# Second norm of the last tile on one engine, four scatters later, and routing products moved by a unit

## The chip, the cores and the metric

The kernel runs on one core of a Trainium2 chip. The metric is the device time of one launch in microseconds (us): the median of the runs before the change is 1239.01 us. The engines are named as the profile names them: PE is TensorE's matrix products (PEld its weight loads), DVE is VectorE, ACT is ScalarE, POOL is GpSimd, and SP is the engine that only issues transfers.

## The reference

One decoder block on 1024 tokens of width 1024, all in float32. The first half normalises, runs a state-space branch and a gated chunk branch, merges them by gates, and projects. The second half, in which the change lies, is a mixture of 32 experts in 4 groups of 8:

```python
h   = x + gate_a * (merged @ w_out)          # output projection and residual
xn  = rmsnorm(h) * (1 + scale_m) + shift_m   # the second norm
lg  = xn @ w_rg + b_rg                       # 4 group logits per token
grp = argmax(lg)                             # one group per token
le  = (xn @ w_re + b_re)[grp]                # 8 expert logits of that group
top_v, top_i = top_k(le, 2)                  # two experts per token
wgt = softmax(lg)[grp] * softmax(top_v)
y   = sum over the two of wgt * ((silu(xn @ w1) * (xn @ w3)) @ w2)
out = rmsnorm(h + gate_m * y)
```

The reference sorts the 2048 pairs of token and expert by expert, in blocks of up to 128 rows.

## The kernel before

The tokens are 8 tiles of 128. The order of the work is written by hand: a list of units, each with its matrix products; before a unit's products, every side generator in flight is advanced by one `yield`. So a `yield` puts what follows it one unit later. There is no scheduler that moves anything; each engine runs its instructions in the order in which they were issued.

The **output projection** (`out_mm`, products of lines L112 to L114: three products of rounded halves for each float32 product) runs tile after tile. A tile has two halves of 512 columns of 24 products each. Tiles 2 to 5 have two units each (one per half), tile 6 four units of 12 products, tile 7 eight units of 6. When a half is complete, `out_read` adds it to the residual on VectorE (h, L87), and `h_half` squares it on ScalarE (L1340) and multiplies it by a row on GpSimd (L87, xn<-h). After the second half, `norm2` joins the side generators.

**norm2(j)** turns the tile by PE transposes (L1355; ScalarE copies them, L105), forms the reciprocal root r on VectorE, and multiplies the turned tile by the router's weights (L1372: the 36 logits). For the rows themselves it scales by r on ScalarE (L1375, two halves) and adds the shift on GpSimd (L87, xn<-xn, two halves), and ScalarE's queue stores the rows to DRAM (L1377, xrows), from where the experts gather them.

**route(tiles)** runs once for each pair of tiles in `GROUPS`: VectorE finds the group, the two experts and a mask `mb` from the logits; after WAIT[0] yields PE forms the running count of each expert (L1464, L1466, L1467), which needs the mask; VectorE and GpSimd form one-hot rows (`ohr`); after WAIT[1] yields PE multiplies them (L1493), and VectorE adds the result to the table of lists in SBUF and keeps the column sums (`cum`). Last, `scatter` writes one row for each choice and token to a table in DRAM by four indirect transfers of GpSimd (L1507). For the last pair the scatters are put in `late_rows` and issued after the third gather of the experts. That table is read only by a loop for overflowing experts at the end of the kernel.

**The experts** start with two gathers of rows (L1675) and the turn of the first of them (L1690), then the third gather, then `late_rows`. Sixteen experts have up to 128 rows and sixteen up to 64; their weights come from DRAM by loads of up to 2 MB (wexp), are rounded by ScalarE (L108, ewh) and completed by VectorE (L87, ewl).

Of the kernel before, what the change touches and what calls it, by code (L numbers as in the profile page):

```python
# [14 lines left out]
AF = mybir.ActivationFunctionType  # L15
OP = mybir.AluOpType
# [8 lines left out]
NJ = 8  # L25
# [27 lines left out]
def hybrid_block(ctx: ExitStack, tc: tile.TileContext, ins, out):  # L53
    nc = tc.nc
    V, A, G, T = nc.vector, nc.scalar, nc.gpsimd, nc.tensor
# [15 lines left out]
    def k4(nm, shape, dt=F32):  # L71
        return pool.tile([P] + shape, dt, name=name(nm), tag="k4", bufs=N4)
# [4 lines left out]
    def tmp(nm, shape, dt=F32, bufs=2):  # L77
        return pool.tile(shape, dt, name=name(nm), tag=nm, bufs=bufs)
# [4 lines left out]
    def ps_aux():  # L83
        return psum.tile([P, 512], F32, name=name("aux"), tag="aux", bufs=4)

    def tt(o, a, b, op, eng=V):
        eng.tensor_tensor(out=o, in0=a, in1=b, op=op)  # L87

    def stt(o, a, s, b, op0, op1, **kw):
        V.scalar_tensor_tensor(out=o, in0=a, scalar=s, in1=b, op0=op0, op1=op1, **kw)  # L90

    def ts(o, a, s1, s2=None, op0=OP.mult, op1=None, eng=V):
        if op1 is None:
            eng.tensor_scalar(out=o, in0=a, scalar1=s1, scalar2=None, op0=op0)
        else:
            eng.tensor_scalar(out=o, in0=a, scalar1=s1, scalar2=s2, op0=op0, op1=op1)
# [7 lines left out]
    def act_copy(o, a):  # L104
        A.activation(out=o, in_=a, func=AF.Copy)  # L105
# [34 lines left out]
    def rsqrt(o, a, n):  # L140
        for _ in rsqrt_steps(o, a, n):
            pass
# [898 lines left out]
    rowv = {}  # L1041
# [272 lines left out]
    def load_next(q=nc.sync, later=None):  # L1314
        if loaded[0] < len(order):
            key = loads[loaded[0]]
            raws[key] = w_load(key[0], expert_of(key[1]), q, whole[key], later, not is_l(key[1]), key)
            loaded[0] += 1
# [27 lines left out]
    def norm2(j):  # L1346

        ht, x2 = hts[j], x2s[j]
        tiles = next(g for g in GROUPS if j in g)
        B = len(tiles)  # L1350

        def turn(hf):
            ps = ps_aux()
            for k in range(4):
                T.transpose(ps[:, k * P:(k + 1) * P], hres[j][:, (4 * hf + k) * P:(4 * hf + k + 1) * P], ident)  # L1355
            o = ht[:, 4 * hf:4 * hf + 4].rearrange("p k c -> p (k c)")
            if j == NJ - 1 and hf == 0:
                V.tensor_copy(out=o, in_=ps)
            else:
                act_copy(o, ps)  # L1360

        turn(0)
        ms, r = nrm[:, j, 3:4], nrm[:, j, 4:5]
        ts(nrm[:, j, 2:3], nrm[:, j, 0:1], 1.0 / DM, RMS_EPS, OP.mult, OP.add)
        stt(ms, nrm[:, j, 1:2], 1.0 / DM, nrm[:, j, 2:3], OP.mult, OP.add)
        rsqrt(r, ms, 1)
        yield
        turn(1)
        yield
        lps = ps_aux()  # L1370
        for k in range(KD):
            T.matmul(out=lps[:, 0:36], lhsT=ht[:, k], rhs=rk["wr"][:, k], start=(k == 0), stop=(k == KD - 1))  # L1372
        for hf in range(2):
            hs = slice(hf * 512, (hf + 1) * 512)
            A.activation(out=x2[:, hs], in_=x2[:, hs], func=AF.Identity, scale=r)  # L1375
            tt(x2[:, hs], x2[:, hs], rowv[3][:, hs], OP.add, G)
        nc.scalar.dma_start(out=xrows[j * P:(j + 1) * P, :], in_=x2)  # L1377
        if j == NJ - 1:
            load_next(nc.scalar, nc.gpsimd)
        yield  # L1380
        if j == tiles[0]:
            groups[tiles] = k4("rt", [DM])
        L = groups[tiles][:, 0:36 * B].rearrange("p (t n) -> p t n", t=B)
        stt(L[:, j - tiles[0]], lps[:, 0:36], r, rk["cb"], OP.mult, OP.add)
        if j == tiles[-1]:
            yield from route(tiles, L)

    late_rows = []
    WAIT = {(4, 5): (2, 2), (6,): (4, 2)}
    GROUPS = ((0, 1), (2, 3), (4, 5), (6, 7))  # L1390

    def route(tiles, L):
# [63 lines left out]
        tt(mb, mk[:, 0], mk[:, 1], OP.add)  # L1456
        for _ in range(WAIT.get(tiles, (1, 1))[0]):
            yield
# [26 lines left out]
        for q, t in pairs:  # L1485
            gts(rhs[:, q, t, 0], mk[:, q, t], ids[:, t:t + 1])
            ts(oh[:, q, t], rk["iota"], pos[:, q, t:t + 1], None, OP.is_equal)
            ts(rhs[:, q, t, 1], mk[:, q, t], wv[:, q, t:t + 1], None, OP.mult)
        for _ in range(WAIT.get(tiles, (1, 1))[1]):
            yield  # L1490
# [14 lines left out]
        def scatter():  # L1505
            for q, t in pairs:
                ins_ = G.indirect_dma_start(out=table[:, :], out_offset=bass.IndirectOffsetOnAxis(ap=adi[:, q, t:t + 1], axis=0),  # L1507
                                            in_=row[:, q, t], in_offset=None, bounds_check=NT * NEXP - 1, oob_is_err=False)
                for prev in scatters:
                    tc.declare_no_dep(ins_.ins, prev.ins, reason="each token and choice has its own row")  # L1510
                scatters.append(ins_)
        for t in range(B):
            tt(cum, cum, mb[:, t], OP.add)
        if tiles[-1] >= NJ - 2:
            late_rows.append(scatter)
        else:
            scatter()
# [13 lines left out]
    def out_read(j, n):  # L1531
        ns = slice(n * 512, (n + 1) * 512)
        tt(hres[j][:, ns], hres[j][:, ns], ops[j, n], OP.add)
        h_half(j, n)
        if n == 1:
            h_store(j)
            side.append(norm2(j))
# [440 lines left out]
    with tc.For_i(0, n_any, 1):  # L1978
        y_add(x_index(NEXP - 1), yos[NEXP - 1][:, 0:512], hbuf_h)
        with tc.For_i(0, NEXP, 1) as e:  # L1980
            n_0 = nc.values_load(sm["sti"][:, bass.ds(e, 1)], min_val=1, max_val=2, skip_runtime_bounds_check_because=why)
            n_b = nc.values_load(nxi[0:1, bass.ds(e, 1)], min_val=1, max_val=NB, skip_runtime_bounds_check_because=why)
            with tc.For_i(n_0, n_b, 1) as b:
                tcol = tmp("tcol", [P, 2], I32, bufs=1)
                for h in range(2):
                    nc.sync.dma_start(out=tcol[HALF * h:HALF * (h + 1)],
                                      in_=tview[bass.ds(b, 1), :, bass.ds(e, 1), :].rearrange("b p e w -> p (b e w)"))
                xi = tmp("xi", [P, 1], I32, bufs=1)
                hf = tmp("hf", [P, 1], bufs=1)
# [55 lines left out]
```

## Time and profile before

| what | value |
|---|---|
| median of 3 runs | 1239.01 us (1237.97 to 1239.11) |
| profiled execution | 1239.78 us, its span 1238.1 us |
| granted TensorE clock, mean | 0.965 |
| PE busy | 1133.7 us, 92% of the span |
| DVE busy | 735.2 us, 59% |
| ACT busy | 463.2 us, 37% |
| POOL busy | 377.6 us, 30% |
| DMA, mean | 253 GB/s |

Times in the rows are microseconds from the start of the span. A row in order of time has the start, the duration, the engine, the line, the operation with its output and inputs, and the number of instructions that were joined to it; in brackets stands how long the engine was idle before and what released it. [...] The output projection ends at 647.7 us; from 666.58 us the experts run.

### The profile page before, as it was taken

What the parts mean: (1) busy time and instruction counts of PE and PEld (TensorE: products, weight loads), DVE (VectorE), ACT (ScalarE), POOL (GpSimd) and SP (SyncE); (2) the same over time, 40 slices, a digit from 0 to 9 for tenths busy, and PEclk for the clock granted to TensorE, in tenths of its full rate; (3) what the DMA queues carried; (4) which work ended last, traced back from release to release, by engine and by line L of the source; (5) the groups of instructions that cost most, each with busy time, mean ns of one, the idle gap of its engine ahead of it and who ended that gap; (6) DMA issues with size and microseconds to landing.
All of it is one profiled execution on the core that took longest, in us unless ns stands there. A gap on an engine that the chain in (4) does not pass through costs nothing. (4 is left out here: it accounts for less than half of the span.)

```text
span 1238.1 us, 16769 instructions
## 1 busy us (share of the span) xinstructions
PE 1133.7 (92%) x6237; PEld 872.7 (70%) x6238; DVE 735.2 (59%) x1223; ACT 463.2 (37%) x664; POOL 377.6 (30%) x477
## 2 busy tenths in 40 slices
PE   4998999999999999999995999999898999898980
PEld 4897888888878888788774776666565666665630
DVE  4614562568597555656668976666464566565616
ACT  6422233234215421034324754444342444443303
POOL 2799273533000211415565111111111111111210
PEclk9999999999999999999897999999899998999995
DMA  9711122583541155545466999999999999998986
GB/s 333 222 35 58 62 86 57 197 289 102 190 151 52 35 190 175 185 166 219 152 229 241 339 353 396 401 402 404 406 400 404 388 397 377 380 394 310 381 301 271
DMA packets 106663, 313.44 MB, mean 253 GB/s; under 512 B 21035, under 2 KB 59527, under 8 KB 91858
## 3 DMA queue, kind: packets, MB, share of 16 engines
q1 hardware_dynamic: 92520, 274.14, 58.6%
q0 software_dynamic: 9088, 20.32, 6.3%
q10 hardware_dynamic: 4970, 17.88, 3.7%
q8 instruction: 50, 0.82, 0.3%
q14 instruction: 35, 0.29, 0.1%
HBM read 287.02 MB, written 33.83 MB: 259 GB/s over the span
## 5 line engine op out<-in xcount | busy, mean ns | idle before, releaser
L87 DVE TENSOR_TENSOR ewl<-wexp,ewh 128x1024 fp32r<-128x1024 f32 x176 | 207.8, 1221 | 82.0 <-ACT ewh L108 79.8
L108 ACT ACTIVATE ewh<-wexp 128x1024 fp32r<-128x1024 f32 x176 | 174.3, 1053 | 38.8 <-DMA wexp<-in_w 36.3
L112 PE MATMUL mm<-xn,wh 128*128 128x512 f32 x320 | 127.4, 398 | 0.0
L114 PE MATMUL mm<-xn,wl 128*128 128x512 f32 x320 | 125.1, 391 | 0.0
L113 PE MATMUL mm<-xn,wh 128*128 128x512 f32 x320 | 125.0, 391 | 0.0
L87 DVE TENSOR_TENSOR wl<-wraw,wh 128x1024 fp32r<-128x1024 f32 x38 | 55.0, 1456 | 110.5 <-ACT wh L108 110.5
L1741 PE MATMUL mm<-wexp,xs 128*64 128x256 f32 x992 | 115.4, 382 | 3.9 <-DMA wexp<-in_w 3.6
L1675 POOL DMA_INDIRECT xg<-xrows,w x29 | 30.7, 1060 | 282.8 <-PE aux L1690 128.6
L113 PE MATMUL mm<-ewl,xth 128*128 128x512 f32 x256 | 103.2, 403 | 0.7 <-DVE ewl L87 0.7
L1741 PEld LDWEIGHTS mm<-wexp,xs 128*64 128x64 f32 x992 | 69.0, 137 | 48.9 <-issue 9.1
L112 PE MATMUL mm<-ewh,xth 128*128 128x512 f32 x256 | 102.3, 400 | 0.2 <-ACT xth L108 0.2
L114 PE MATMUL mm<-ewh,xtl 128*128 128x512 f32 x256 | 100.5, 393 | 0.0
L1725 POOL DMA_INDIRECT hbuf<-yo,w x28 | 52.8, 1887 | 123.1 <-DVE yo L87 109.7
L798 ACT ACTIVATE gate<-mm,vcol 128x512 f32<-128x512 f32 x32 | 22.0, 688 | 134.7 <-PE mm L114 134.7
L112 PE MATMUL mm<-ewh,w 128*128 128x512 f32 x128 | 55.9, 437 | 17.7 <-ACT ewh L108 17.7
L112 PEld LDWEIGHTS mm<-xn,wh 128*128 128x128 f32 x320 | 60.4, 189 | 13.7 <-issue 1.6
L114 PEld LDWEIGHTS mm<-xn,wl 128*128 128x128 f32 x320 | 60.2, 188 | 12.8
L113 PEld LDWEIGHTS mm<-xn,wh 128*128 128x128 f32 x320 | 60.4, 189 | 11.8
L87 DVE TENSOR_TENSOR yo<-mm,macc 128x512 f32<-128x512 f32 (+1 forms) x64 | 42.7, 686 | 41.6 <-PE mm L1741 37.5
L108 ACT ACTIVATE w<-aux 128x512 fp32r<-128x512 f32 x16 | 9.6, 597 | 140.5 <-PE aux L1709 140.5
L113 PEld LDWEIGHTS mm<-ewl,xth 128*128 128x128 f32 x256 | 48.3, 189 | 19.3 <-DVE ewl L87 10.1
L108 ACT ACTIVATE wh<-wraw 128x1024 fp32r<-128x1024 f32 x38 | 39.6, 1052 | 58.6 <-PE mm L113 29.6
(369 smaller groups left out, 2454.1 us busy)
## 6 DMA issues: line engine op xcount, KB each, us to landing
wexp<-in_w SPq DMA_DIRECT2D x76, 2048.0 KB, 25.5
wexp<-in_w SPq DMA_DIRECT2D x48, 512.0 KB, 12.0
wadr<-in_w_ada SPq DMA_DIRECT2D x32, 512.0 KB, 4.8
wexq<-in_w SPq DMA_DIRECT2D x24, 512.0 KB, 9.1
wada<-in_w_ada SPq DMA_DIRECT2D x8, 1024.0 KB, 11.2
wraw<-in_w_gate SPq DMA_DIRECT2D x16, 512.0 KB, 3.8
gate<-gate ACTq DMA_DIRECT2D x16, 512.0 KB, 2.8
gin<-gate SPq DMA_DIRECT2D x16, 512.0 KB, 3.8
```

The source lines that it names most:

```text
L87: eng.tensor_tensor(out=o, in0=a, in1=b, op=op)
L108: A.activation(out=hi, in_=raw, func=AF.Copy)
L112: T.matmul(out=ps, lhsT=lh, rhs=rh, start=first, stop=False)
L113: T.matmul(out=ps, lhsT=lh, rhs=rl, start=False, stop=False)
L114: T.matmul(out=ps, lhsT=ll, rhs=rh, start=False, stop=last)
L798: A.activation(out=box["g"][:, sl], in_=box[hf], func=AF.Sigmoid, bias=col("bg", 8 * s + d))
L1675: G.indirect_dma_start(out=xg, out_offset=None, in_=rows[:, :], in_offset=bass.IndirectOffsetOnAxis(ap=xi, axis=0), bounds_check=rows.shap ...
L1725: G.indirect_dma_start(out=rows[:, :], out_offset=bass.IndirectOffsetOnAxis(ap=yi, axis=0), in_=yo, in_offset=None, bounds_check=rows.shap ...
L1741: T.matmul(out=ps[sl, 0:n], lhsT=xt[:, k, HALF * h:HALF * (h + 1)], rhs=w[:, n * g:n * (g + 1)], start=(kt == 0), stop=(kt == nk - 1), til ...
```

## The change

Three edits. The last tile's second norm is finished by one VectorE operation, (x2 * r) + shift over 128x1024, in place of two scalings on ScalarE and two adds on GpSimd. The entry of WAIT for the pair (2, 3) is new: its running-count products come one unit later and its one-hot products two; the one-hot products of the pair (4, 5) come one unit later. (The entry for (6,) named no group and had no effect.) The four scatters of the pair (4, 5) join those of the pair (6, 7) in `late_rows`.

```diff
--- before.py
+++ after.py
@@ -1370,10 +1370,14 @@
         lps = ps_aux()
         for k in range(KD):
             T.matmul(out=lps[:, 0:36], lhsT=ht[:, k], rhs=rk["wr"][:, k], start=(k == 0), stop=(k == KD - 1))
-        for hf in range(2):
-            hs = slice(hf * 512, (hf + 1) * 512)
-            A.activation(out=x2[:, hs], in_=x2[:, hs], func=AF.Identity, scale=r)
-            tt(x2[:, hs], x2[:, hs], rowv[3][:, hs], OP.add, G)
+        if j == NJ - 1:
+
+            stt(x2, x2, r, rowv[3], OP.mult, OP.add)
+        else:
+            for hf in range(2):
+                hs = slice(hf * 512, (hf + 1) * 512)
+                A.activation(out=x2[:, hs], in_=x2[:, hs], func=AF.Identity, scale=r)
+                tt(x2[:, hs], x2[:, hs], rowv[3][:, hs], OP.add, G)
         nc.scalar.dma_start(out=xrows[j * P:(j + 1) * P, :], in_=x2)
         if j == NJ - 1:
             load_next(nc.scalar, nc.gpsimd)
@@ -1386,7 +1390,7 @@
             yield from route(tiles, L)
 
     late_rows = []
-    WAIT = {(4, 5): (2, 2), (6,): (4, 2)}
+    WAIT = {(2, 3): (2, 2), (4, 5): (2, 3)}
     GROUPS = ((0, 1), (2, 3), (4, 5), (6, 7))
 
     def route(tiles, L):
@@ -1511,7 +1515,7 @@
                 scatters.append(ins_)
         for t in range(B):
             tt(cum, cum, mb[:, t], OP.add)
-        if tiles[-1] >= NJ - 2:
+        if tiles[-1] >= NJ - 4:
             late_rows.append(scatter)
         else:
             scatter()
```

Behind the first edit all line numbers are 4 higher: L1464 becomes L1468, L1493 L1497, L1507 L1511.

On PE the running-count products of the pair (2, 3) stood directly behind tile 5's last product, ahead of the logits of tile 4. Before (mm is a projection product, rt_4968 the pair's routing buffer, ht a turned tile):

```order
2386 L114 MATMUL mm_5104<-wo_4431,ml_4839 128x512
2387 L1464 LDWEIGHTS before
2388 L1464 MATMUL aux_5143<-rt_4968,before 128x32
...
2396 L1467 MATMUL aux_5143<-cum,ones 128x32
2397 L1372 MATMUL aux_5171<-rk_2032,ht_4942 128x36 x8
2398 L1355 MATMUL aux_5185<-ident,h_4842 128x128 x4
2399 L112 MATMUL mm_5204<-wo_4100,mh_5005 128x512
```

And after:

```order
2386 L114 MATMUL mm_5104<-wo_4431,ml_4839 128x512
2387 L1372 MATMUL aux_5141<-rk_2032,ht_4942 128x36 x8
2388 L1355 MATMUL aux_5155<-ident,h_4842 128x128 x4
2389 L112 MATMUL mm_5174<-wo_4100,mh_5005 128x512
...
2400 L114 MATMUL mm_5174<-wo_4100,ml_5006 128x512
2401 L1468 LDWEIGHTS before
2402 L1468 MATMUL aux_5189<-rt_4968,before 128x32
...
2410 L1471 MATMUL aux_5189<-cum,ones 128x32
2411 L1355 MATMUL aux_5219<-ident,h_4842 128x128 x4
2412 L112 MATMUL mm_5174<-wo_4431,mh_5005 128x512
```

The logits of tile 4, a turn of tile 5 and twelve products of tile 6 now come first.

On ScalarE, in the same place: rt_4968 is again the pair's routing buffer, xn_685 the rows of tile 4, ht_5071 the turned tile 5, mh the rounded half of the projection's input. Before:

```order
334 L108 ACTIVATE mh_5133<-mg_3879 128x1024
335 L1459 ACTIVATE rt_4968<-rt_4968 128x8
336 L1460 ACTIVATE rt_4968<-rt_4968 128x2
337 L1375 ACTIVATE xn_685_4941<-xn_685_4941,nrm 128x512 x2
338 L1377 DMA xrows<-xn_685_4941 128x1024
339 L105 ACTIVATE ht_5071<-aux_5185 128x512
340 L105 ACTIVATE ht_5071<-aux_5242 128x512
```

And after:

```order
334 L108 ACTIVATE mh_5133<-mg_3879 128x1024
335 L1379 ACTIVATE xn_685_4941<-xn_685_4941,nrm 128x512 x2
336 L1381 DMA xrows<-xn_685_4941 128x1024
337 L105 ACTIVATE ht_5071<-aux_5155 128x512
338 L1463 ACTIVATE rt_4968<-rt_4968 128x8
339 L1464 ACTIVATE rt_4968<-rt_4968 128x2
340 L105 ACTIVATE ht_5071<-aux_5219 128x512
```

The two exponentials of the pair moved behind the scaling and the store of tile 4 and the first copy of turned tile 5; they now stand between its two copies.

On GpSimd, from the pair (2, 3)'s one-hot rows on (ohr_5149 before, ohr_5195 after); xn_685 are the rows of tile 4, xn_698 of tile 5, xn_715 before and xn_714 after those of tile 6, table the scatters. Before:

```order
286 L94 TENSOR_SCALAR ohr_5149<-rt_4968,rk_2032 128x32 x4
287 L87 TENSOR_TENSOR xn_685_4941<-xn_685_4941,macc_2838 128x512 x2
288 L1507 DMA table<-rk_2032,rt_4968 32768x2 x4
289 L87 TENSOR_TENSOR xn_715_5261<-h_5009,macc_2174 128x512
290 L87 TENSOR_TENSOR xn_698_5070<-xn_698_5070,macc_2838 128x512 x2
291 L87 TENSOR_TENSOR xn_715_5261<-h_5009,macc_2174 128x512
292 L94 TENSOR_SCALAR ohr_5366<-rt_5240,rk_2032 128x32 x4
293 L87 TENSOR_TENSOR xn_715_5261<-xn_715_5261,macc_2838 128x512 x2
294 L1507 DMA table<-rk_2032,rt_5240 32768x2 x4
295 L87 TENSOR_TENSOR xn_733_5479<-h_5137,macc_2174 128x512 x2
```

And after:

```order
286 L87 TENSOR_TENSOR xn_685_4941<-xn_685_4941,macc_2838 128x512 x2
287 L94 TENSOR_SCALAR ohr_5195<-rt_4968,rk_2032 128x32 x4
288 L87 TENSOR_TENSOR xn_714_5238<-h_5009,macc_2174 128x512
289 L87 TENSOR_TENSOR xn_698_5070<-xn_698_5070,macc_2838 128x512 x2
290 L1511 DMA table<-rk_2032,rt_4968 32768x2 x4
291 L87 TENSOR_TENSOR xn_714_5238<-h_5009,macc_2174 128x512
292 L94 TENSOR_SCALAR ohr_5366<-rt_5217,rk_2032 128x32 x4
293 L87 TENSOR_TENSOR xn_714_5238<-xn_714_5238,macc_2838 128x512 x2
294 L87 TENSOR_TENSOR xn_733_5467<-h_5137,macc_2174 128x512 x2
295 L94 TENSOR_SCALAR ohr_5555<-rt_5429,rk_2032 128x32 x4
```

The adds of tile 4 moved ahead of the one-hot rows, the pair (2, 3)'s scatters behind the adds of tile 5; the pair (4, 5)'s scatters and the adds of the last tile (xn_733) are gone from here.

## Rows read from the trace of the kernel before

**Rows 1.** TensorE's waits from 600 to 667 us (the view of waits).

```profile
PE aux L1464 <- DVE rt L87: 9.4, 3, 6.3
...
PE aux L1493 <- DVE ohr L94: 3.0, 2, 1.6
```

**Rows 2.** Stretches: length, busy PE, PEld, DVE, ACT, POOL, clock, DMA, GB/s.

```profile
600.00:620.00 20.00, 17.38 (x86) 14.99 (x84) 16.91 (x76) 5.50 (x12) 7.79 (x9) 0.83 0.53 188
...
640.00:650.00 10.00, 9.66 (x44) 7.68 (x42) 3.40 (x10) 2.02 (x5) 6.24 (x6) 0.86 0.78 279
```

**Rows 3.** TensorE in time: start, duration, operation, count, [idle before <-releaser].

```profile
592.10 1.87 PE L1372 MATMUL aux<-rk,ht 128*128 128x36 f32 x16
...
608.44 0.18 PE L1464 MATMUL aux<-rt,before 128*128 128x32 bf16 x1 [2.62 <-DVE rt L87]
...
608.57 3.46 PE L1372 MATMUL aux<-rk,ht 128*128 128x36 f32 x16
...
630.54 0.18 PE L1464 MATMUL aux<-rt,before 128*128 128x32 bf16 x1 [0.45 <-DVE rt L87]
...
637.93 1.43 PE L1493 MATMUL aux<-ohr 128*128 128x64 f32 x8 [1.57 <-DVE ohr L94]
...
639.51 0.63 PE L113 MATMUL mm<-wo,mh 128*128 128x512 f32 x1
...
647.27 0.39 PE L113 MATMUL mm<-wo,mh 128*128 128x512 f32 x1
647.50 0.40 PE L114 MATMUL mm<-wo,ml 128*128 128x512 f32 x1
...
666.58 1.94 PE L1690 MATMUL aux<-ident,xg 128*128 128x128 f32 x8 [5.38 <-DMA xg<-xrows,xidx]
```

**Rows 4.** VectorE in order of time, operations of the routing.

```profile
605.46 0.34 DVE L87 TENSOR_TENSOR rt<-rt,rk 128x8 f32<-128x8 f32 x2
...
605.97 0.42 DVE L87 TENSOR_TENSOR rt<-rt 128x8 f32<-128x8 f32 x3
...
624.01 4.48 DVE L87 TENSOR_TENSOR rt<-rt 128x8 f32<-128x8 f32 x3
...
652.75 1.37 DVE L87 TENSOR_TENSOR rt<-rt,rk 128x8 f32<-128x8 f32 x2
...
654.30 1.20 DVE L87 TENSOR_TENSOR rt<-rt 128x8 f32<-128x8 f32 x3
```

**Rows 5.** ScalarE and its queue in order of time, around 615 us.

```profile
615.08 0.33 ACTq L1377 DMA_DIRECT2D xrows<-xn  x1
615.51 0.60 ACT L105 ACTIVATE ht<-aux 128x512 f32<-128x512 f32 x1 [3.40 <-POOL xn L87]
```

**Rows 6.** GpSimd in order of time.

```profile
612.55 2.50 POOL L87 TENSOR_TENSOR xn<-xn,macc 128x512 f32<-128x512 f32 x2
...
652.77 2.50 POOL L87 TENSOR_TENSOR xn<-xn,macc 128x512 f32<-128x512 f32 x2 [2.57 <-ACT xn L1375]
...
671.51 1.01 POOL L1507 DMA_INDIRECT table<-rk,rt  x1 [0.30 <-DVE rk L90]
...
683.02 1.04 POOL L1675 DMA_INDIRECT xg<-xrows,w  x1 [6.87 <-PE aux L1690]
697.71 1.01 POOL L1675 DMA_INDIRECT xg<-xrows,w  x1 [13.65 <-PE aux L1690]
```

**Rows 7.** Transfers: issue, count, size, median us to landing.

```profile
wexp<-in_w SPq DMA_DIRECT2D x76, 2048.0 KB, 25.5
...
wexp<-in_w POOLq DMA_DIRECT2D x1, 2048.0 KB, 11.6
```

**Rows 8.** The view of the tile table, its scatters' landing.

```profile
DMA to landing us min/median/max: 2.1/5.5/8.8
```

**Rows 9.** The view of line L90 (ns min/median/max), operations of 128x1024.

```profile
L90 DVE SCALAR_TENSOR_TENSOR tail<-tail,nrm,gf x8: 1279/1280/1287, 1215.4 to 1228.5; 128x1024 f32<-128x1024 f32 x8
```

**Rows 10.** TensorE's waits from 666 to 1215 us, the largest.

```profile
PE mm L112 <- ACT ewh L108: 17.7, 8, 3.4
```

## Prediction

> **What bounds the kernel now.** I read four views, in this order. First the waits of TensorE from 600 to 667 us [rows 1]: the end of the output projection, the routing of the last tokens and the first gather. Until then TensorE runs its products back to back, so what delays it here delays the end. The reader is to see that 9.4 us go to three waits of the running-count products (L1464) for the routing mask and 3.0 us to two waits of the one-hot products (L1493). Second the table by stretches [rows 2]: beside these waits the granted clock is lost, 0.83 in 600:620 and 0.86 in 640:650, so part of each is at the lower of its two levels. Third TensorE's rows in order of time [rows 3], which tie the two together: the 2.62 us wait at 608.44 is followed by a logit product of 3.46 us where the same one took 1.87, and the 1.57 us wait at 637.93 by products of 0.63 (639.51) where they are 0.39 otherwise and start 0.23 apart (647.27, 647.50). The wait of 0.45 at 630.54 has no such tail. Fourth the rows of VectorE, ScalarE and GpSimd around these places [rows 4 to 6].
>
> After 667 us TensorE waits little: the largest item is 17.7 us for the experts' rounded weights, over 8 times [rows 10]. Loads there follow one another as buffers come free, so I take this stage to move as one block with the moment at which the first gathered rows are turned (666.58, [rows 3]). The prediction is then: how much earlier that moment comes.
>
> **The change part by part.**
>
> *Pair (2,3): its running-count products a unit later, its one-hot products two.* The 2.62 us wait at 608.44 goes, since by then twelve products stand ahead of them; the mask was ready at 608.4, and TensorE now arrives at about 610.6 (605.66, plus 1.7 for the logits, 0.4 for the turn, 12 x 0.23). With it goes the half-clock stretch behind it: 3.46 - 1.87 = 1.6 for the logits, about 0.4 for the turn, and six products of 0.63 like the one at 639.51, each some 0.2 more, = 1.2; together 3.2. So -5.8.
>
> What is late next: the logits of tile 5. They need ScalarE's copies of the turned tile, and these stand behind tile 4's store of its normed rows, which waits for GpSimd's two adds. In the trace the adds start at 612.55, after four one-hot rows of GpSimd [rows 6]; the store is issued at 615.08, and the copy runs at 615.51 [rows 5]. The change puts the adds ahead of the one-hot rows, so they should end at 613.9 to 614.5; then the store's issue (0.33), one copy (0.60), the two small exponentials that now stand between the copies (0.3, an estimate), and the second copy (0.6): 615.7 to 616.4. TensorE would be there at 610.65 + 0.4 + 2.75 = 613.8. A new wait of 1.9 to 2.6, or less if the adds overlap better; I take +2.0. I bound it by 0.9 and 2.6 (the wait that went).
>
> Does this wait bring the half clock back? Of the waits shown, 2.62 and 1.57 did, 0.45 did not. 2.0 lies among those that did; its price in rows is between 0 and 3.2. I take half, +1.6. [...]
>
> *Pair (4,5).* Its routing on VectorE comes behind the table update of pair (2,3), and that behind pair (2,3)'s one-hot products, which now run in the second half of tile 6. In the trace this routing lost 4.48 - 0.42 = 4.1 us in three small operations at 624.01, against 605.97 [rows 4], while GpSimd ran three adds of 128x512. These adds now come ahead of the pair's scatters, so most of this loss goes; but the start is held by the one-hot products. By hand: logits of tile 5 done at 617.5, twelve products and the one-hot products to 621.1, table update to 622.5, routing of some 4 to 5 us: the mask at about 627. TensorE arrives at about 625.3. The wait of 0.45 becomes about 1.75 (0 to 2.5): +1.3, from -0.45 to +2.0.
>
> Its one-hot products come six products later, 6 x 0.23 = 1.4 us. Of the 1.57 us wait about 0.5 stays, since the routing in front is no quicker: -1.1 (0 to -1.57). The half clock behind it (8 products x 0.20 = 1.6) goes with it in most cases: -1.3. Together -2.4, bounds +0.5 and -3.2.
>
> *Pair (4,5)'s scatters.* Four issues of 1.01 us, 0.30 apart (the row at 671.51), leave GpSimd before the tail and stand behind the third gather with the four that were there. Eight take 8 x 1.3 = 10.4 us from 670.2 (one spacing before that row) to 680.6. GpSimd's next work is the gather at 683.02, before which it idled 6.87: 2.4 us are left, so nothing. Without that cover each scatter would cost the gather 1.3; and even then its rows are turned only after those of the expert before, whose turn frees GpSimd at 697.71 [rows 6]. [...] In the tail an emptier GpSimd may start its first multiplication 0.3 earlier; I take 0.2, within the next term.
>
> A wait is added: VectorE's logit operation of tile 6 takes the buffer of pair (2,3)'s routing and so waits for that pair's scatters to land. They are issued from about 622 to 627, and the slowest landing in the trace is 8.8 us [rows 8]: 636 at the latest. Queued behind it are pair (4,5)'s table update and the residual adds of the last tile, which are due at about 640. So 4 us are left, and I count nothing.
>
> *The last tile's norm.* Two ScalarE scalings and two GpSimd adds (2.50 from 652.77 [rows 6]) go. They were not on the path themselves; but during the adds VectorE's routing of the last pair took 1.37 for two operations against 0.34, and 1.20 for three against 0.42 [rows 4]: 1.8 us, all of it on the path that ends the last wait of 6.3 [rows 1]. They are replaced by one VectorE operation of 128x1024 ahead of the last logits. The same form takes 1.28 us at the end of the kernel [rows 9], of which I let 0.08 overlap: +1.2. Left: -0.6, with the 0.2 above -0.8; bounds -1.1, and +1.2 if the stalls have another cause. [...]
>
> **The sum.** -5.8 + 2.0 + 1.6 + 1.3 - 2.4 - 0.8 = -4.1 us. The profiled execution took 1239.78 (span 1238.1 and 1.7 around it), so 1235.7 for its like; it lies 0.8 above the median of the runs, 1239.01, so the median after should be 1234.9.
>
> **The rivals.**
>
> 1. *The wait only moves.* The new wait before the logits of tile 5 is as long as the old (2.6), the half clock comes back whole (3.2), pair (4,5)'s wait is 2 longer and its half clock stays: -5.8 + 2.6 + 3.2 + 2.0 - 1.1 - 0.8 = +0.1; with half of these, -2. Time 1237 to 1239. For it: ScalarE's queue did wait 3.40 for GpSimd here [rows 5]. Against it: the four one-hot rows ahead of the adds are gone. Chance 0.26.
>
> 2. *No half clock at all before the last tile.* Waits of 0.9 and 0.5: -5.8 + 0.9 + 0.1 - 3.2 - 0.8 = -8.8; with one wait near 1.8, -7.5. Time about 1231.5. For it: a shorter wait left the clock alone. Against it: the copies stand behind the store in a fixed order. Chance 0.17.
>
> 3. *Slower: the landing of pair (2,3)'s scatters holds VectorE.* It decides from the point where they land after about 640. The scatters seen landed in 8.8 at most, but the weights' loads take 25.5 in the median [rows 7]. Issued until 627 and landing 25 later gives 652: VectorE would begin the residual adds of the last tile 5 to 6 us after they were done in the trace, and the tail would end 3 to 5 later: about 1243. Chance 0.05; with it I count 0.03 for the new VectorE operation coming on top of waits that stay (+2.5 or more).
>
> 4. *The gain is taken back by the experts.* The weights' loads, 25.5 us each, would end when they did, and the 17.7 us of waits for rounded weights [rows 10] would grow by most of the gain: about 1238.5. Against it: most of the loads start when TensorE frees a buffer, so they start earlier too. Chance 0.05.
>
> The forecast keeps 0.44.
>
> **How the numbers follow.** What a measurement of this kernel can tell from no change is about 0.2%, 2.5 us. Of the forecast's 0.44 nearly all (0.41) and the whole of rival 2 (0.17) are beyond that, and of rival 1 some 0.06: faster 0.64. The same: the rest of these and rival 4, 0.28. Slower 0.08. The range: down to rival 2's 1231, up to a little over the old median, where rivals 1 and 4 end: 1231 to 1239.6. The forecast's own is 1233 to 1237.
>
> **What would show it.** Right: no wait at the first running-count products near 608 and no clock of 0.5 from 608 to 615; a wait of about 2 us before the logits of tile 5 near 614 to 616; the last product of the projection at about 644 where it was 647.50; 1.03 and 0.78 us missing from VectorE's last routing, and one operation of 1.28 in front of it; the first turn of gathered rows at about 662.5. Wrong: a wait on the scatters' landing in VectorE's queue before 640, a half clock behind both new waits, or a turn that comes 4 us earlier and an end that does not.

## The result and the profile after

The changed kernel takes 1231.13 us (median of 6 runs, 1229.40 to 1234.27) where the kernel before took 1238.38 (6 runs beside them): ratio 0.9947, 95% interval 0.9937 to 0.9958. Run again later beside the parts it took 1231.6 against 1238.01, ratio 0.9947 (0.9933 to 0.9961). So it is 6.4 to 7.3 us faster: the forecast's sign, and at the edge of the range (1234.9, 1231.0 to 1239.6). It lies outside the forecast's own part of that range (1233 to 1237) and near what the prediction's second rival gave (1231.5). The profiled execution after has a span of 1230.9 us.

TensorE's waits from 600 to 662 us in the profile after, against [rows 1] (engine, line waited at, what released it: us in total, times, longest; the first gathered rows are turned at L1694):

```profile
PE aux L1468 <- DVE rt L87: 6.6, 2, 5.4
PE aux L1694 <- DMA xg<-xrows,xidx: 5.5, 1, 5.5
PE aux L1497 <- DVE ohr L94: 2.0, 2, 1.3
...
PE aux L1372 <- ACT ht L105: 0.2, 1, 0.2
```

The running-count products wait twice and not three times, the one-hot products 2.0 us and not 3.0. A wait at the logits (L1372) is new, of 0.2 us. The stretches that answer to [rows 2]:

```profile
600.00:620.00 20.00, 19.82 (x114) 16.65 (x113) 16.20 (x71) 6.68 (x16) 7.96 (x10) 1.00 0.54 188
...
640.00:650.00 10.00, 5.21 (x34) 4.27 (x32) 7.96 (x36) 2.25 (x6) 3.14 (x4) 0.88 0.99 403
```

From 600 to 620 the granted TensorE clock, given as a share of full speed, is whole: 1.00 for 0.83. In 640:650 the 0.88 belongs to the tail behind the projection, which now ends at 642: the clock reads 1.00 in 640:642 and 642:647, and 0.59 in 647:650, where TensorE has no product. TensorE in order of time, against [rows 3]:

```profile
601.37 0.60 PE L1355 MATMUL aux<-ident,h 128*128 128x128 f32 x4
...
607.30 1.87 PE L1372 MATMUL aux<-rk,ht 128*128 128x36 f32 x16
...
615.91 1.98 PE L1372 MATMUL aux<-rk,ht 128*128 128x36 f32 x16 [0.18 <-ACT ht L105]
...
627.37 0.18 PE L1468 MATMUL aux<-rt,before 128*128 128x32 bf16 x1 [1.15 <-DVE rt L87]
...
629.86 1.87 PE L1372 MATMUL aux<-rk,ht 128*128 128x36 f32 x16
...
635.21 1.43 PE L1497 MATMUL aux<-ohr 128*128 128x64 f32 x8 [0.64 <-DVE ohr L94]
...
642.03 0.60 PE L1355 MATMUL aux<-ident,h 128*128 128x128 f32 x4
...
660.05 1.94 PE L1694 MATMUL aux<-ident,xg 128*128 128x128 f32 x8 [5.47 <-DMA xg<-xrows,xidx]
```

The wait of 2.62 us and the 3.46 us logits behind it are gone: each of the three logits here takes 1.87 to 1.98. Pair (4,5)'s products wait 1.15 and 0.64 us. The first turn of tile 7 stands directly behind the projection's last product: 642.03, where it was 647.73. The first gathered rows are turned at 660.05, where it was 666.58.

To compare executions I use three stretches of each profile: from tile 4's second turn (599.73 before, 601.37 after; the expectations call it the first turn of tile 5) to the first turn of tile 7 (**projection**), from there to the first turn of gathered rows (**tail**), and from there to the end (**experts**). The two turns in the profile before:

```profile
599.73 0.60 PE L1355 MATMUL aux<-ident,h 128*128 128x128 f32 x4
...
647.73 0.60 PE L1355 MATMUL aux<-ident,h 128*128 128x128 f32 x4
```

Before: 48.00, 18.85 and 571.5 us. After: 40.66, 18.02 and 570.9. So the change gave 7.3 us in the projection and 0.8 in the tail, and the experts took the same within their spread (567.8 to 571.5 in all profiles of this study, 569.3 in a second one of the kernel before).

The 7.3 us can be split. TensorE's waits in the projection, the short ones at the turns with them, add up to 4.96 us before and 2.30 after. Without them the projection takes 43.0 us before and 38.4 after. It also takes 38.4 without its waits in the three other profiles that have no half-clock product and the same order of products as the changed kernel (after2, e12_waits and e6_no_norm below). So about 2.7 us came from shorter waits, and about 4.7 from the half clock that no longer follows them.

The moment at which the projection begins lies 1.6 us later in the profile after; before it the two kernels run the same work. It lay between 599.2 and 602.4 in the profiles of this study. In part this is a stretch of half clock near 563 to 570 us (in 566:568 the clock reads 0.50 after and 1.00 before): the four profiles without it have 599.2 to 599.7, the ten with it 599.4 to 602.4. That is why single executions are compared by stretches and kernels by the runs.

### The profile page after: what moved, and what is told of

Its sections match the earlier page's. It is cut to its first block, busy times and chain, and to the rows that moved or that the text cites. A ratio compares the mean times of both kernels' runs of the same rounds, so it can differ in the third digit from the quotient of the medians.

```text
span 1230.9 us, 16767 instructions
## 1 busy us (share of the span) xinstructions
PE 1130.5 (92%) x6237; PEld 869.6 (71%) x6238; DVE 730.8 (59%) x1224; ACT 461.7 (38%) x662; POOL 377.2 (31%) x475
```

## Experiments

In the order of the argument; each run is named with its time and its ratio to the kernel before from the same session. The first two rows are the executions of the section above. A product counts as half-clock when its row has 0.63 us and not 0.39; in the profile before the clock reads 0.50 in 640:642, among the first kind, and 1.00 in 644:647, among the second. In windows of 1 us that profile has 1.00 in 1142 of 1230 and 0.50 in 67; the other 21 lie between.

| run | what it has of the change | projection, us | half-clock products in it | tail, us | median, us | ratio (95%) |
|---|---|---|---|---|---|---|
| before | nothing | 48.00 | 12 | 18.85 | 1238.38 | |
| after | all | 40.66 | 0 | 18.02 | 1231.13 | 0.9947 (0.9937 to 0.9958) |
| before2 | nothing | 47.25 | 10 | 18.95 | (1237.85, one) | |
| e1_wait23 | pair (2,3) | 43.52 | 7 | 18.71 | 1234.75 | 0.9983 (0.9969 to 0.9997) |
| e2_wait45 | pair (4,5) | 44.35 | 7 | 19.81 | 1237.68 | 1.0003 (0.9991 to 1.0016) |
| e3_late | scatters | 46.26 | 7 | 18.85 | 1237.55 | 1.0000 (0.9988 to 1.0011) |
| e4_norm | norm | 47.18 | 13 | 18.17 | 1238.21 | 1.0003 (0.9989 to 1.0017) |
| e12_waits | both pairs | 41.30 | 0 | 19.61 | 1233.72 | 0.9967 (0.9955 to 0.9979) |
| e23_wait45_late | pair (4,5), scatters | 44.12 | 5 | 18.95 | 1234.38 | 0.9971 (0.9960 to 0.9983) |
| e6_no_norm | all but the norm | 41.17 | 0 | 18.88 | 1231.59 | 0.9946 (0.9930 to 0.9961) |
| after2 | all | 41.42 | 0 | 18.08 | 1231.60 | 0.9947 (0.9933 to 0.9961) |
| e7_wait33 | all, pair (4,5) later still | 40.29 | 0 | 18.10 | 1230.62 | 0.9946 (0.9929 to 0.9964) |
| e5_held_store | all, a store held | 44.75 | 14 | 18.20 | 1233.03 | 0.9957 (0.9943 to 0.9970) |
| e8_both | both of these | 41.31 | 3 | 18.22 | 1229.79 | 0.9935 (0.9922 to 0.9949) |

The theory behind all of them: the four edits work on one chain, TensorE's waits with the half clock that follows them. The rival: each edit gives its own few tenths or microseconds, and they add up.

**before2**, the kernel before once more.

> The kernel before, one more profile. Theory A (the wait at pair (2,3)'s running-count products is in every execution, the half clock behind it in most, but not at a fixed place): a wait of 1.8 to 2.7 us there, and from the first turn of tile 5 to that of tile 7 46 to 48 us, with at least one stretch of half clock. Theory B (the profile of before showed a rare case): a wait under 1.5 us or under 44 us for the stretch.

```profile
608.71 0.19 PE L1464 MATMUL aux<-rt,before 128*128 128x32 bf16 x1 [1.97 <-DVE rt L87]
...
608.84 3.61 PE L1372 MATMUL aux<-rk,ht 128*128 128x36 f32 x16
```

As Theory A had it: the wait is 1.97 us, the logits behind it are at half clock (3.61), and a second stretch follows pair (4,5)'s one-hot products. The first profile was no rare case.

**e1_wait23**

```diff
-    WAIT = {(4, 5): (2, 2), (6,): (4, 2)}
+    WAIT = {(2, 3): (2, 2), (4, 5): (2, 2)}
```

> The kernel before with one entry of the change, pair (2,3) at (2,2); pair (4,5) stays at (2,2), the norm and the scatters are as before. Theory A (most of the gain is the wait of 2.6 us at pair (2,3)'s running-count products and the half-clock stretch of 3.2 us behind it, and neither comes back): 4 to 5 us faster, no clock of 0.5 between 605 and 635, and pair (4,5)'s one-hot products wait about 2.0 us (0.64 in the changed kernel plus the six products of 1.4 us that no longer stand ahead of them). Theory B (the wait moves to the logits of tile 5 and brings the half clock with it): within 2 us of the kernel before, with a wait over 1.4 us at those logits and a clock of 0.5 behind it.

TensorE in order of time:

```profile
615.04 1.98 PE L1372 MATMUL aux<-rk,ht 128*128 128x36 f32 x16 [0.98 <-ACT ht L105]
...
617.97 0.63 PE L112 MATMUL mm<-wo,mh 128*128 128x512 f32 x1
...
635.05 1.43 PE L1493 MATMUL aux<-ohr 128*128 128x64 f32 x8 [1.99 <-DVE ohr L94]
```

The kernel is 3.3 us faster by the medians and 2.1 by the ratio, between Theory A's 4 to 5 and Theory B's 2; the projection is 4.5 us shorter than in the first profile before and 3.7 shorter than in before2. Pair (4,5)'s one-hot products wait 1.99 us, as Theory A said. But the wait did move to tile 5's logits (0.98), and a stretch of half clock stands behind it here, from 617.2, when the logits had run at full clock. Theory A excluded that. The edit alone does not make this place safe.

**e2_wait45**

```diff
-    WAIT = {(4, 5): (2, 2), (6,): (4, 2)}
+    WAIT = {(4, 5): (2, 3)}
```

> The kernel before with pair (4,5) at (2,3): its one-hot products six projection products later; nothing else. Theory A (the wait of 1.57 us and the half clock behind it, 1.6 us, both go): 2.5 to 3 us faster, wait at these products under 0.3 us, granted clock in 640:650 near 1.00 up to the end of the projection. Theory B (the half clock there comes from elsewhere, or the delay is met again at the last tile): 0 to 1.4 us faster.

```profile
638.98 1.43 PE L1493 MATMUL aux<-ohr 128*128 128x64 f32 x8 [0.21 <-DVE ohr L94]
```

The wait at the one-hot products is 0.21 us and the half clock behind them is gone: the projection is 3.65 us shorter than in the first profile before, 2.9 shorter than in before2. But the runs show nothing (1.0003). About 0.9 of it was given back in the tail, 19.81 us for 18.85 and 18.95; why the runs show none of the other 2 to 2.7 us stays open. GpSimd and VectorE in the tail:

```profile
645.56 0.97 POOL L1507 DMA_INDIRECT table<-rk,rt  x1 [0.30 <-issue]
646.54 2.50 POOL L87 TENSOR_TENSOR xn<-h,macc 128x512 f32<-128x512 f32 x2
```

```profile
647.48 1.59 DVE L90 SCALAR_TENSOR_TENSOR nrm<-nrm 128x1 f32<-128x1 f32 x1
```

The last scatter now ends at 646.5, when tile 7's first residual add has been done for 1.2 us (it ran from 644.63, 0.69). GpSimd's two multiplications start only then. VectorE's mean operation runs beside them, ends with them at 649.1, and takes 1.59 us. In the profile before it took 0.81:

```profile
649.41 0.81 DVE L90 SCALAR_TENSOR_TENSOR nrm<-nrm 128x1 f32<-128x1 f32 x1
```

**e3_late**

```diff
-        if tiles[-1] >= NJ - 2:
+        if tiles[-1] >= NJ - 4:
```

> The kernel before with pair (4,5)'s four scatters among the late ones; nothing else. Theory A (they cost nothing where they stood and are covered where they go): 0 to 0.4 us faster, from GpSimd's first multiplication of the last tile that follows the residual add at once. Theory B (an emptier GpSimd before the tail is a real part of the 7 us): 1.5 us faster or more. If eight scatters in a row hold the gather behind them and TensorE needs it: slower by 1 to 3 us.

No difference in the runs or in the tail: alone the edit is worth nothing, as Theory A said. Its profile shows something else:

```profile
609.78 0.18 PE L1464 MATMUL aux<-rt,before 128*128 128x32 bf16 x1 [1.83 <-DVE rt L87]
...
609.90 1.95 PE L1372 MATMUL aux<-rk,ht 128*128 128x36 f32 x16
...
616.90 1.43 PE L1493 MATMUL aux<-ohr 128*128 128x64 f32 x8 [1.84 <-DVE ohr L94]
```

Waits of 1.83 and 1.84 us, and the logits between them take 1.95: no half clock behind either. The second of these waits is not there before, where the slower products behind the first wait brought TensorE to this place late enough. So the projection is only 1.0 to 1.7 us shorter than in the two profiles before, although the half clock of that place is missing.

**e4_norm**: the first edit of the change alone.

```diff
+        if j == NJ - 1:
+            stt(x2, x2, r, rowv[3], OP.mult, OP.add)
+        else:
...
```

> The kernel before with the last tile's second norm in one VectorE operation; nothing else. Theory A (the 1.8 us by which GpSimd's two adds held VectorE's last routing go, the operation costs 1.2): 0.6 us faster, and VectorE's two joined rows take 0.34 and 0.42 us where they took 1.37 and 1.20. Theory B (the two stalls had another cause): 1.2 us slower. Theory C (the earlier store of the last rows brings the first gather forward too): 1.5 to 2 us faster.

The tail is 18.17 us, 0.68 shorter; the runs can't show that (1.0003). Theory A's size.

**e12_waits**: the change's line of WAIT alone.

```diff
-    WAIT = {(4, 5): (2, 2), (6,): (4, 2)}
+    WAIT = {(2, 3): (2, 2), (4, 5): (2, 3)}
```

> The kernel before with both entries of WAIT, scatters and norm as before. Theory A: the projection from the first turn of tile 5 to the first turn of tile 7 takes 40.7 us as in the changed kernel (48.0 before), but pair (4,5)'s scatters now end after tile 7's residual add, GpSimd's two multiplications run joined behind them, VectorE's mean operation (nrm, 0.81 before) takes 1.5 us or more, and the stretch from there to the first turn of gathered rows is 19.8 us or more (18.85 before): 5.5 to 6 us faster in all. Theory B (no such link): the stretch stays at 18.85 and the kernel is 3.7 (the sum of the two parts measured) or 7 us faster.

```profile
599.39 0.60 PE L1355 MATMUL aux<-ident,h 128*128 128x128 f32 x4
...
640.69 0.60 PE L1355 MATMUL aux<-ident,h 128*128 128x128 f32 x4
```

```profile
642.37 1.59 DVE L90 SCALAR_TENSOR_TENSOR nrm<-nrm 128x1 f32<-128x1 f32 x1
```

Both halves of Theory A are there: the projection is 41.30 us with no half-clock product, and the tail is 19.61, 0.8 longer than before, with 1.59 us for the mean operation. But the kernel is 4.3 us faster and not 5.5 to 6: by the time alone it is nearer to Theory B's 3.7, the sum of what the two entries gave one by one (3.3 and 0.4).

**e23_wait45_late**

```diff
-    WAIT = {(4, 5): (2, 2), (6,): (4, 2)}
+    WAIT = {(4, 5): (2, 3)}
...
-        if tiles[-1] >= NJ - 2:
+        if tiles[-1] >= NJ - 4:
```

> The kernel before with pair (4,5) at (2,3) and its scatters among the late ones. Theory A (with the products later, the scatters run into tile 7's residual add; 0.96 us of the tail in the run with (2,3) alone are theirs): the stretch from the first turn of tile 7 to the first turn of gathered rows is 18.85 us and not 19.81, VectorE's mean operation takes 0.6 to 0.8 us and not 1.59; about 1 us faster than with (2,3) alone. Theory B (the longer tail there has another cause): 19.5 us or more.

```profile
644.65 2.58 POOL L87 TENSOR_TENSOR xn<-h,macc 128x512 f32<-128x512 f32 x2 [6.65 <-DVE h L87]
```

```profile
646.67 0.58 DVE L90 SCALAR_TENSOR_TENSOR nrm<-nrm 128x1 f32<-128x1 f32 x1
```

GpSimd now starts with the residual add. The tail is back at 18.95, and the mean operation takes 0.58. The run is 3.3 us faster than e2_wait45 by the medians, and the intervals of the two ratios do not overlap. So the scatters' edit, worth nothing where the products come early, is worth about 0.9 us in the tail once they come late. The same edit between e12_waits and e6_no_norm below gives 0.7 us in the tail and 2.1 by the medians, there with overlapping intervals. What the runs show beyond the tail's share stays open.

The wait at pair (2,3)'s running count is still there in this kernel, and the half clock behind it too:

```profile
608.96 0.18 PE L1464 MATMUL aux<-rt,before 128*128 128x32 bf16 x1 [1.99 <-DVE rt L87]
...
609.08 3.53 PE L1372 MATMUL aux<-rk,ht 128*128 128x36 f32 x16
```

**e6_no_norm**: the changed kernel with the old norm of the last tile.

```diff
-        if j == NJ - 1:
-            stt(x2, x2, r, rowv[3], OP.mult, OP.add)
-        else:
...
```

> The changed kernel with the last tile's second norm as before. Theory A: 0.6 to 0.8 us slower than the changed kernel, 6.2 to 6.8 faster than the kernel before; the stretch from the first turn of tile 7 to the first turn of gathered rows 18.7 us (18.02 in the changed kernel). Theory B (the norm is the part that carries the rest): 2 us slower than the changed kernel or more.

VectorE's two rows of the last routing:

```profile
647.15 1.38 DVE L87 TENSOR_TENSOR rt<-rt,rk 128x8 f32<-128x8 f32 x2
...
648.70 1.20 DVE L87 TENSOR_TENSOR rt<-rt 128x8 f32<-128x8 f32 x3
```

1.38 and 1.20 us: the stalls of [rows 4] are back, and the tail is 18.88 for 18.02 and 18.08. In the runs this kernel and the changed one can't be told apart (1231.59 and 1231.60).

**after2**, the changed kernel beside them.

> The changed kernel again, beside the parts. Theory A (the four edits work together: 7 us are the same here): 6.5 to 7.5 us faster than the kernel before, no half clock between 605 and 640, a wait between 0.2 and 1.4 us at the logits of tile 5. Theory B (the 7 us came from the runs with which it was compared, the edits only add up): 3.5 to 4.5 us faster, what the four edits gave one by one (3.3, 0.4, 0.5 and -0.1 by the medians).

6.4 us by the medians. One by one the four edits gave 3.3, 0.4, 0.5 and -0.1, together 4.1; by the ratios the four together give 1.4, against 6.6 here. So in the runs they come to less one by one than together; by the medians the gap is 2.3 us, not much more than the uncertainty of one run. The profiles show one link between the edits, in the tail: the scatters count only with the later products. In the projection they show none: the entries of WAIT alone shorten it by 4.5 and 3.65 us, and both together by 6.7. The rest of the gap is not explained. The wait at tile 5's logits is 0.93 us here, 0.18 in the first profile; neither has half clock behind it.

**e7_wait33**

```diff
-    WAIT = {(2, 3): (2, 2), (4, 5): (2, 3)}
+    WAIT = {(2, 3): (2, 2), (4, 5): (3, 3)}
```

> The changed kernel with pair (4,5) at (3,3): its running-count products and its one-hot products six projection products later each. Theory A (the waits that are left there, 1.15 and 0.64 us, are only early arrivals of TensorE): both go, 1.5 to 1.8 us faster than the changed kernel, 8.5 faster than the kernel before. Theory B (VectorE, which then updates the table later, is late for the last tile): 0 to 0.5 us faster, the time comes back in front of the last pair's products.

```profile
627.93 0.66 PE L1355 MATMUL aux<-ident,h 128*128 128x128 f32 x4 [1.74 <-DVE nrm L96]
```

The waits at pair (4,5)'s products are gone, but tile 6's second turn waits 1.74 us, since VectorE's residual add of that tile stands behind the pair's routing. The projection is 0.4 us shorter than in the first profile after and 1.1 shorter than in after2, and the runs show no clear difference (ratios 0.9946 and 0.9947): mostly Theory B, though the time comes back one step later and not at the last tile.

**e5_held_store**: tile 4's store of its rows is issued behind ScalarE's second copy of turned tile 5.

```diff
-        nc.scalar.dma_start(out=xrows[j * P:(j + 1) * P, :], in_=x2)
+        def store():
+            nc.scalar.dma_start(out=xrows[j * P:(j + 1) * P, :], in_=x2)
+        if j == 4:
+            held.append(store)
+        else:
+            store()
...
         turn(1)
+        while held:
+            held.pop()()
         yield
```

> The changed kernel with tile 4's store of its rows issued behind ScalarE's second copy of turned tile 5, not ahead of the first. Theory A (the wait of 0.2 to 0.9 us at the logits of tile 5 is the store's wait for GpSimd's adds): no wait there, 0.2 to 0.9 us faster than the changed kernel up to the first turn of tile 7, unless it is met again at pair (4,5)'s running-count products. Theory B (the copies wait for something else): the same wait.

TensorE in order of time (logits now L1375, running count L1476, one-hot L1505):

```profile
613.37 1.87 PE L1375 MATMUL aux<-rk,ht 128*128 128x36 f32 x16
...
625.77 0.18 PE L1476 MATMUL aux<-rt,before 128*128 128x32 bf16 x1 [2.20 <-DVE rt L87]
...
628.92 3.46 PE L1375 MATMUL aux<-rk,ht 128*128 128x36 f32 x16
...
637.46 1.12 PE L1505 MATMUL aux<-ohr 128*128 128x64 f32 x8
```

The wait at the logits is gone, so it was the store's. But TensorE now reaches pair (4,5)'s running count earlier and waits 2.20 us, and a long stretch of half clock follows: logits of 3.46 us, 14 products at 0.63. The projection is 3.3 us longer than in after2. The runs are not faster: the median is 1.4 us above that of after2, with overlapping intervals. This is the prediction's first rival, the wait that only moves and brings the clock with it, one place further on.

**e8_both**: e5_held_store's edit and pair (4,5) at (3,3).

> The changed kernel with tile 4's store held as in the run e5_held_store and pair (4,5) at (3,3). Theory A (VectorE's routing of pair (4,5), which starts only after pair (2,3)'s one-hot products, is the last bound here; it moves with them): the wait of 1.74 us at the second turn of tile 6 stays, all before it comes 0.7 us earlier: 1 to 1.5 us faster than the changed kernel, 7.5 to 8.5 faster than the kernel before. Theory B (nothing is left to gain in this stretch): the time of the changed kernel.

```profile
626.16 1.12 PE L1356 MATMUL aux<-ident,h 128*128 128x128 f32 x4 [2.54 <-DVE nrm L96]
...
629.50 1.96 PE L1375 MATMUL aux<-rk,ht 128*128 128x36 f32 x16
```

The one wait left is longer than forecast (2.54 us at the second turn of tile 6), with a short stretch of half clock behind it (the turn takes 1.12; the logits at 629.50 are at full clock again), and the projection is that of the changed kernel. By the medians it is the fastest kernel run, 1229.79, and 8.3 us faster than the kernel before, as Theory A had it. But its interval (0.9922 to 0.9949) overlaps that of the changed kernel, and its projection is no shorter: it is not shown to be better, and Theory A's reason is not shown.

## Why the prediction was right in sign and small in size

*Pair (2,3), -5.8.* Held. The wait at 608 and the half clock behind it are gone in all eight profiles of kernels that have this entry of WAIT. The price was right too: the half clock of the kernel before, here and behind pair (4,5)'s one-hot products, was priced at 3.2 and 1.6, and the split above gives 4.7 for both.

*The new wait before the logits of tile 5, +2.0.* The place and its cause were right (e5_held_store removes it), its size was not: 0.18 and 0.93 us. ScalarE in the profile after, against [rows 5]:

```profile
614.84 0.33 ACTq L1381 DMA_DIRECT2D xrows<-xn  x1
615.26 0.60 ACT L105 ACTIVATE ht<-aux 128x512 f32<-128x512 f32 x1 [2.93 <-POOL ohr L94]
...
615.95 0.59 ACT L105 ACTIVATE ht<-aux 128x512 f32<-128x512 f32 x1
```

The store was issued at 614.84 and the first copy ended at 615.86; the logits began at 615.91 and ran beside the second copy. (The profile names GpSimd's one-hot rows as what ended the wait before the copy; they began when the adds ended, at 614.8, and the store waits for the adds.) The sum had put both copies and the exponentials in front of the logits, about 1 us too much. The 0.18 of the first profile against 0.69 to 0.98 in the five others with this order comes from further up: VectorE, from which this chain starts, waits there before tile 6's split of the projection's input (ml), here in after2 for pair (0,1)'s scatters to land:

```profile
602.37 1.23 DVE L87 TENSOR_TENSOR ml<-mg,mh 128x1024 fp32r<-128x1024 f32 x1 [6.77 <-DMA table<-rk,rt]
...
605.43 0.69 DVE L87 TENSOR_TENSOR h<-h,mm 128x512 f32<-128x512 f32 x1
```

The wait ends at tile 4's second turn there (602.37 and 602.35); in the first profile it ended 0.72 us ahead of it (600.65 and 601.37), which is nearly the 0.75 between the two waits. The wait at the logits and the lead of this split over the turn add up to 0.90 us in the first profile (0.18 and 0.72) and to 0.91 in after2 (0.93 and -0.02).

*The half clock behind that wait, +1.6.* This is the term that decided the size: it measured 0. Not one half-clock product stands in the projection of after, after2, e12_waits, e6_no_norm or e7_wait33. Without it the sum is -5.7, and with a wait of 0.9 instead of 2.0, -6.8. This was in part luck: the rows did not tell whether a wait of 0.9 us is followed by half clock, and in e1_wait23 one of 0.98 at this very place was. For waits near 2 us the runs show both (last section).

*Pair (4,5).* The wait at its running count became 1.15 (+0.7; forecast +1.3), the one at the one-hot products 0.64 and its half clock went (-2.5; forecast -2.4). VectorE's three small operations of that routing, the 4.48 us of [rows 4], take 0.48. The three adds of GpSimd that ran beside them before (624.42 to 628.23) now end at 623.34, ahead of them:

```profile
624.83 0.48 DVE L87 TENSOR_TENSOR rt<-rt 128x8 f32<-128x8 f32 x3
...
646.05 1.29 DVE L90 SCALAR_TENSOR_TENSOR xn<-xn,nrm,macc 128x1024 f32<-128x1024 f32 x1
...
648.00 0.34 DVE L87 TENSOR_TENSOR rt<-rt,rk 128x8 f32<-128x8 f32 x2
...
648.51 0.42 DVE L87 TENSOR_TENSOR rt<-rt 128x8 f32<-128x8 f32 x3
```

*The last tile's norm, -0.6.* Held: 1.29 us for the new operation, 0.34 and 0.42 for the rows that were 1.37 and 1.20, and 0.68 to 0.86 us of the tail (e4_norm against before, the two profiles of the changed kernel against e6_no_norm). The prediction put the stalls down to GpSimd's two adds, and the runs agree: in e6_no_norm, where these adds run from 647.17 to 649.67, the two rows beside them take 1.38 and 1.20 again. Whether the new operation is also longer beside GpSimd's adds was not tested: it ran from 646.05, and GpSimd was idle from 644.3 to 649.4.

*The scatters.* Nothing alone, as forecast; but the forecast had not seen that the later products of pair (4,5) would push those scatters into the tail, where e2_wait45 and e12_waits are 0.8 to 1.0 us longer than before. In the sum this edit is a condition of the other one. The eight late scatters were covered, by less than forecast:

```profile
667.58 2.31 POOL L1511 DMA_INDIRECT table<-rk,rt  x1 [0.30 <-issue]
...
674.10 1.97 POOL L1511 DMA_INDIRECT table<-rk,rt  x1 [0.31 <-issue]
676.95 1.05 POOL L1679 DMA_INDIRECT xg<-xrows,w  x1 [0.89 <-PE aux L1694]
```

Two of them took 2.31 and 1.97 us, and the idle time before the next gather, 6.87 in [rows 6], is 0.89. TensorE still released that gather, so they cost nothing. This cover is not certain: an estimate from these rows is that a third scatter of about 2 us, where the others take about 1, would have used up the 0.89.

*The added wait on the scatters' landing* (rival 3) did not show: VectorE's logit operation of tile 6 ran without a gap behind the one-hot rows in both profiles of the changed kernel (at 636.00 and 637.75). *The experts* (rival 4) took 570.9 and 569.2 us after, 571.5 and 569.3 before: the gain was not taken back.

The chance of 0.17 for the second rival was too low: its first condition, a short wait at the logits, was the likely one with the copies counted rightly (0.18 to 0.98 us in six profiles). Its second, no half clock behind that wait, held in five of these six.

## What to carry to other kernels

When a wait is removed, follow TensorE to the next place where it will be early, and price the clock there too. In this kernel the half clock behind the waits cost more than the waits, 4.7 us against 2.7, and one moved store turned a harmless wait of 0.9 us into one of 2.2 with 14 products at half clock. Test edits together as well as one by one; three of these four measured nothing alone, and one is worth something only because another pushes it into the tail. In front of a consumer that works in steps, count only the first piece it needs: in the profile after the logits began at 615.91 and the second copy at 615.95.

## What the runs showed of the hardware

Between about 1 and 2 us a wait's length alone did not decide, in these profiles, whether half clock follows. Waits of 1.99 (e23_wait45_late, 608.96), 1.97 (before2) and 1.57 us (before) were followed by it, and so was one of 0.98 (e1_wait23, 617.97). Those of 1.99 (e1_wait23, 635.05), 1.84 and 1.83 (e3_late), 1.74 (e7_wait33) and 1.15 (after) were not. Outside that band the projections show one outcome each: half clock came with the waits of 2.20 (e5_held_store), 2.54 (e8_both) and 2.62 us (before), and with none of 0.93 or less. What else decides was not tested. The same work before the change's place also had or lacked a half-clock stretch from one execution to the next, near 563 to 570 us: of the kernel before, the first profile has none and before2 has one from 565.4 to 567.9. In the profile after it begins at 565.6, and TensorE has no wait between 516.59 and there.
